# Dealing the gelu passes 2, 3, 3, 0 over the head pairs, and moving y's first low parts behind the third pair's scores

## The chip, the cores and the metric

The kernel runs on one core of one Trainium2 chip. The metric is the device time of one execution in microseconds (us); the median of the runs is compared. The engines are named as the profile names them: PE (TensorE), DVE (VectorE), ACT (ScalarE), POOL (GpSimd) and SP, whose queue issues most of the transfers.

## The reference

A two-layer trunk over 1024 tokens of width 1024, all in float32. The change lies in layer 0, which runs two branches from one input projection:

```python
proj = h @ w_in                      # h = rmsnorm(x)
u_s5, g_s5, q, k, v, g_ret = split(proj)
y = s5(u_s5)                         # diagonal state-space layer, 8 blocks of channels
y = gelu(y)
y = y * sigmoid(y @ glu_w + glu_b)   # the GLU
y_s5 = y * silu(g_s5)
# retention: 8 heads, chunks of 64, per head normalised
scores = einsum('nihd,njhd->nhij', q, k) * decay
out = scores @ v + (q * q_dec) @ S   # S: the state before the chunk
y_ret = norm(out) * silu(g_ret)
x = x + concat(y_s5, y_ret) @ w_out
```

Layer 1 is a convolution module (two projections with a gate, a causal convolution of width 31, a layer norm, an output projection) and a final norm.

## The kernel before

Products keep float32 accuracy by splitting each operand into a high part, rounded for PE, and a low part, the rest. A matmul of 128x128 by 128x512 is issued three times (lines L270 to L272): high by high, high by low, low by high. The high parts are ACT copies, the low parts are subtractions on DVE or POOL.

The program writes the work in one order with priorities, and a scheduler places every instruction in the static order of its engine. A block under `issue_after(x)` is placed behind x; it is a rule for the order. Each engine then runs its list in that order, and waits on semaphores where an operand isn't there. A tile with `bufs=n` gives its next use a free buffer only when the use n before it has been read.

After the front of layer 0 (u, gates, the S5 layer) come four pairs of heads. For a pair, `ret_heads` does: transposes of k (`ktp`) and their decay (`kt`, L1084); products of keys and values (`kv`) and their running state `S` (L1109, L1111), which DVE updates; scores (`sp`, L1118), which DVE masks into `sc` (L1124); products `ro` of q with S (L1145) and of sc with values (L1150); the norm of each head (`st`, `mv`, `rs`, `on`, L1159 to L1165); transposes back (`rt`, L1173); the gate (`grl`, loaded at L1133, multiplied at L1176); and a store to DRAM (`yr_d`, L1179). The k and q projections of the next pair (`mm_k`, `mm_q`), their swapped copies (`kswp`, `qswp`, loaded at L985) and their rotation on POOL and DVE (`krot`, `qrot`) lie between.

Beside the heads the S5 output takes the gelu, in eight passes of 128 channels each (`y_pass`, L919 to L922): a load of `yp` from DRAM on the SP queue, the gelu into `yn` on ACT with its reordering, and a store to `yn_d` issued by ACT. Both tiles have one buffer. Passes 0 and 1 stand with the first pair; 2 and 3, 4 and 5, and 6 and 7 with the next three, each behind the square roots (`rs`) of the pair before.

The GLU then reads y again, in two halves of the tokens. `load_split` loads two blocks of 128 channels into one tile of three buffers (`yf`, L1214), ACT casts the high part (`yh`, L1183), and DVE subtracts the low part (`yl`, L1185). The low parts of the first half (h = 0) are free to go at once; those of the second half stand behind kt of the last pair (the first six blocks) and its masked scores (the last two). For each of the eight output blocks and each half, the GLU loads the S5 gate (`yg`, L1234) and y again (`yn`, L1236), multiplies them on POOL (L1237), runs 24 matmuls (`mm_glu`), a tanh on ACT and a product on DVE (L1242). The scheduler puts the first of these matmuls between the products of the third and fourth pairs. Behind each step of the GLU stand some pieces of `weight_low` (L225 to L230), which loads half a block of the layer-1 weights w_c, forms its low part, and stores it for later (`lows(3)` after each first half, `lows(1)` after each second half, until 14 are done).

Of the kernel before, what the change touches and what calls it, by code (L numbers as in the profile page):

```python
# [11 lines left out]
F32 = mybir.dt.float32  # L12
# [7 lines left out]
P = 128  # L20
# [37 lines left out]
class Trunk:  # L58
# [856 lines left out]
    def y_pass(self, rp, cb):  # L915

        nc = self.nc
        yt = rp.tile([P, 8, P], F32, name=f"yp_{cb}", tag="yp", bufs=1)
        nc.sync.dma_start(yt[:], self.y_d[cb].rearrange("i h g m -> (h g) i m"))  # L919
        yn = rp.tile([P, P, 8], F32, name=f"yn_{cb}", tag="ynt", bufs=1)  # L920
        nc.scalar.activation(yn[:], yt[:].rearrange("p i m -> p m i"), AF.Gelu_apprx_tanh)
        nc.scalar.dma_start(self.yn_d[cb * P:(cb + 1) * P], yn[:].rearrange("p m i -> p (m i)"))  # L922

    def retention(self, st):
        nc, A = self.nc, self.A
        r0 = self.r0 = self.pool("ret0", 1, stack=st)
        early = ExitStack()
        rq = self.rq = self.pool("retq", 1, stack=early, side="right")
        self.vt = [[(r0 if d else rq).tile([P, 4, HALF], F32, name=f"v{d}_{h}") for h in range(2)] for d in range(2)]
        self.rk = rq.tile([P, 2, T], F32, name="ropek")  # L930
        nc.sync.dma_start(self.rk[:], A["rope_k"])
        self.mask = r0.tile([P, NH, P], F32, name="retmask")
        nc.sync.dma_start(self.mask[:], A["ret_mask"])
        self.g128 = r0.tile([P, 4], F32, name="g128")
        nc.sync.dma_start(self.g128[:], A["ret_g128"])
        self.reps = r0.tile([P, NH], F32, name="reteps")
        nc.sync.dma_start(self.reps[:], A["ret_eps"])
        ahead = None
        for pair in range(4):
            cur = list(ahead or self.ret_proj(pair))[-1]  # L940
            if pair == 0:
                with ExitStack() as vst:
                    V = self.ret_values(self.pool("vp", 1, stack=vst))
                self.rp = self.pool("ret", 1, stack=st)
                self.kdec = self.rp.tile([P, NH, 64], F32, name="kdec")
                nc.sync.dma_start(self.kdec[:], A["ret_kdec"])
                ry = self.pool("rety", 1, stack=early, side="right")
            with ExitStack() as held:
                if pair:
                    held.enter_context(self.tc.issue_after(self.last_rs.ins))  # L950
                for cb in (2 * pair, 2 * pair + 1):
                    self.y_pass(ry, cb)

            def turned():
                if pair == 3:
                    early.close()
                    self.lp = self.pool("l1", side="right")
            ahead = pair in AHEAD and self.ret_proj(pair + 1)
            if ahead:
                next(ahead)  # L960
            self.ret_heads(pair, *cur, V, turned)
# [111 lines left out]
    def ret_heads(self, pair, K, Q, qadds, V, turned):  # L1073
        nc, rp = self.nc, self.rp
        v = nc.vector
# [17 lines left out]
        for hf in range(2):  # L1093
            ps = self.bank(f"kv{hf}_{pair}")
            for b4 in range(4):
                b = 4 * hf + b4
# [6 lines left out]
            for b4 in range(4):  # L1103
                b = 4 * hf + b4
# [21 lines left out]
                    self.mask[:, 2 * pair + hh, :].unsqueeze(1).broadcast_to([P, 4, P]), op=ALU.mult)  # L1126


        gts = []
        for hh in range(2):  # L1130
            h = 2 * pair + hh
            gt = rp.tile([P, T], F32, name=f"grl_{h}", tag="grl", bufs=3)
            nc.sync.dma_start(gt[:], self.gr_d[h * P:(h + 1) * P])  # L1133
            gts.append(gt)
        todo = []
        for hf in range(2):
# [17 lines left out]
            for hh in range(2):  # L1154
                h, ps = 2 * pair + hh, pss[hh]
# [21 lines left out]
        for hh in range(2):  # L1177
            h = 2 * pair + hh
# [8 lines left out]
    def layer0_back_and_layer1(self, st):  # L1187
        nc, A = self.nc, self.A
        v, gp = nc.vector, nc.gpsimd
# [7 lines left out]
        def load_split(src, name, halves):  # L1197
            res = [[], []]

            def put(kb, h, f):  # L1200
                a, b = (self.op_tile(self.opA, f"A{h}", f"{name}{q}{kb}_{h}") for q in "hl")
                self.split(f, a, b, v, None if halves or h == 0 else self.last_kt if kb < 6 else self.masked[0])
                res[h].append((a, b))
            for h in range(2):
                for kb in range(KB):
                    if halves:
                        f = lp.tile([P, HALF], F32, name=f"{name}f{kb}_{h}", tag="tp", bufs=TP)[:]
                        nc.sync.dma_start(f, src[rows(kb), hs(h)])
                    else:

                        if kb % 2 == 0:
                            f2 = self.wp.tile([P, 2, HALF], F32, name=f"{name}f{kb}_{h}", tag="wf", bufs=3)
                        f = f2[:, kb % 2, :]
                        nc.sync.dma_start(f, src[rows(kb), hs(h)])  # L1214
                    put(kb, h, f)
            return res
# [8 lines left out]
        def lows(n):  # L1225
            for k in islice(left, n):
                self.weight_low(lp, k, (("cs", "pilot"), ("cq", "sq")), 1)
        ws = {}

        for nb, h in [(nb, h) for nb in range(6) for h in range(2)] + [(6, 0), (7, 0), (6, 1), (7, 1)]:  # L1230
            if h == 0:
                ws[nb] = self.wnext(f"glu{nb}")
            yg = lp.tile([P, HALF], F32, name=f"yg{nb}_{h}", tag="ld", bufs=2)
            nc.sync.dma_start(yg[:], self.gs_d[rows(nb), hs(h)])  # L1234
            yn = lp.tile([P, HALF], F32, name=f"yn{nb}_{h}", tag="ev", bufs=3)
            nc.sync.dma_start(yn[:], self.yn_d[rows(nb), hs(h)])  # L1236
            gp.tensor_tensor(yg[:], yg[:], yn[:], op=ALU.mult)  # L1237
            ps = self.bank(f"mm_glu{nb}_{h}", aux=False)
            self.gemm(ps[:], ws[nb], ys_in[h])
            sg = lp.tile([P, HALF], F32, name=f"sg{nb}_{h}", tag="u", bufs=5)  # L1240
            nc.scalar.activation(sg[:], ps[:], AF.Tanh, scale=0.5, bias=hgb[:, nb:nb + 1])
            v.scalar_tensor_tensor(sg[:], sg[:], 1.0, yg[:], op0=ALU.add, op1=ALU.mult)  # L1242
            if h == 0:
                a, b = (self.op_tile(opB, "B0", f"ys{q}{nb}") for q in "hl")
                nc.scalar.mul(a[:], sg[:], 0.5)
                glu_end = v.scalar_tensor_tensor(b[:], sg[:], 0.5, a[:].bitcast(F32), op0=ALU.mult, op1=ALU.subtract)
                ys0[nb], sg0[nb] = (a, b), sg
                lows(3)
                continue
            yr1 = lp.tile([P, HALF], F32, name=f"yr1_{nb}", tag="tp", bufs=TP)  # L1250
            nc.sync.dma_start(yr1[:], self.yr_d[rows(nb), hs(1)])
            t3f[nb], t2f[nb] = (opB.tile([P, HALF], F32, name=f"{n}_{nb}", tag="B1") for n in ("t3f", "t2f"))
            v.scalar_tensor_tensor(t3f[nb][:], sg[:], -0.5, yr1[:], op0=ALU.mult, op1=ALU.add)
            glu_end = v.scalar_tensor_tensor(t2f[nb][:], sg0.pop(nb)[:], 0.5, t3f[nb][:], op0=ALU.mult, op1=ALU.add)
            lows(1)

        def operand(name, tag, f):
            a, b = (self.op_tile(opB if tag[0] == "B" else self.opA, tag, f"{name}{q}") for q in "hl")
# [498 lines left out]
```

## Time and profile before

| | us |
|---|---|
| median of three runs | 1200.46 |
| lowest and highest of them | 1195.26, 1200.8 |
| the profiled execution | 1199.91 |
| its span, from the first to the last instruction | 1198.1 |
| PE busy in the span | 1167.2 |
| DVE, POOL, ACT busy | 941.0, 687.4, 554.3 |

The granted clock of PE is 0.995 over the span. In the profile a row of a timeline gives start, length, engine, line, operation, output and inputs, the number of instructions merged, and in brackets the idle time before it with what ended it. Line numbers are those of the kernel before.

### The profile page before, as it was taken

What the parts mean: (1) busy time and instruction counts of PE and PEld (TensorE: products, weight loads), DVE (VectorE), ACT (ScalarE), POOL (GpSimd) and SP (SyncE); (2) the same over time, 40 slices, a digit from 0 to 9 for tenths busy, and PEclk for the clock granted to TensorE, in tenths of its full rate; (3) what the DMA queues carried; (4) which work ended last, traced back from release to release, by engine and by line L of the source; (5) the groups of instructions that cost most, each with busy time, mean ns of one, the idle gap of its engine ahead of it and who ended that gap; (6) DMA issues with size and microseconds to landing.
All of it is one profiled execution on the core that took longest, in us unless ns stands there. A gap on an engine that the chain in (4) does not pass through costs nothing.

```text
span 1198.1 us, 17522 instructions
## 1 busy us (share of the span) xinstructions
PE 1167.2 (97%) x6150; PEld 967.8 (81%) x6150; DVE 941.0 (79%) x1529; ACT 554.3 (46%) x833; POOL 687.4 (57%) x489
## 2 busy tenths in 40 slices
PE   8999999999999999988899999999999999999997
PEld 7888878888888888867788888778887887888887
DVE  6875889999617787758788887379999999999643
ACT  7212333332225644233645535367756578444652
POOL 2049979888835133432344034338894678988641
PEclk9999999999999999999999999999999999999999
DMA  9353577788898686664998467866448653456863
GB/s 337 106 182 100 185 265 268 262 275 281 280 299 251 223 280 217 192 211 158 347 325 307 150 228 250 294 229 207 161 152 295 228 178 114 140 188 241 276 247 120
DMA packets 131480, 271.19 MB, mean 226 GB/s; under 512 B 12864, under 2 KB 41792, under 8 KB 131264
## 3 DMA queue, kind: packets, MB, share of 16 engines
q1 hardware_dynamic: 130240, 265.88, 65.8%
q10 hardware_dynamic: 1152, 4.19, 0.9%
q8 instruction: 48, 0.79, 0.3%
q14 instruction: 40, 0.33, 0.1%
HBM read 194.07 MB, written 71.76 MB: 222 GB/s over the span
## 4 chain that ended last, share of the span: by engine, by line
PE 79%; DMA 8%; DVE 7%; POOL 2%; ACT 2%; issue 2%; SPq 1%; DVEq 0%; POOLq 0%; ACTq 0%
PE mm_g L272 7%; PE mm_g L271 7%; PE mm_g L270 6%; PE mm_w L270 3%; PE mm_w L271 3%; PE mm_w L272 3%; PE mm_u L272 2%; PE mm_u L271 2%; PE mm_oc L272 2%; PE mm_oc L270 2%; PE mm_oc L271 2%; PE mm_u L270 2%; PE mm_b L271 2%; PE mm_a L271 2%; PE mm_b L272 2%; PE mm_a L270 2%
## 5 line engine op out<-in xcount | busy, mean ns | idle before, releaser
L1446 DVE SCALAR_TENSOR_TENSOR cv<-u,convw,cv 128x512 f32<-128x512 f32 x358 | 245.2, 748 | 5.7 <-ACT cv L1432 3.9
L1426 POOL TENSOR_TENSOR tp<-tp,tp 128x512 f32<-128x512 f32 x104 | 138.8, 1337 | 33.9 <-ACT tp L1425 28.1
L272 PE MATMUL mm_g<-xh,wl_g 128*128 128x512 f32 x256 | 100.7, 393 | 0.0
L271 PE MATMUL mm_g<-xl,wh_g 128*128 128x512 f32 x256 | 100.6, 393 | 0.0
L270 PE MATMUL mm_g<-xh,wh_g 128*128 128x512 f32 x256 | 100.6, 393 | 0.0
L1425 ACT ACTIVATE tp<-u,convw 128x512 f32<-128x512 f32 x104 | 69.3, 713 | 9.2 <-POOL tp L1426 9.1
L271 PEld LDWEIGHTS mm_g<-xl,wh_g 128*128 128x128 f32 x256 | 48.1, 188 | 11.2 <-issue 1.4
L272 PEld LDWEIGHTS mm_g<-xh,wl_g 128*128 128x128 f32 x256 | 48.1, 188 | 10.4
L270 PEld LDWEIGHTS mm_g<-xh,wh_g 128*128 128x128 f32 x256 | 48.1, 188 | 9.8 <-issue 0.2
L272 PE MATMUL mm_oc<-zh,wl_woc 128*128 128x512 f32 (+1 forms) x152 | 54.7, 360 | 0.1
L270 PE MATMUL mm_oc<-zh,wh_woc 128*128 128x512 f32 (+1 forms) x152 | 54.5, 362 | 0.0
L271 PE MATMUL mm_oc<-zl,wh_woc 128*128 128x512 f32 (+1 forms) x152 | 54.2, 356 | 0.0
L270 PE MATMUL mm_glu<-yh,wh_glu 128*128 128x512 f32 x128 | 50.0, 393 | 2.2 <-ACT yh L1183 2.2
L272 PE MATMUL mm_g<-h1h,wl_cg 128*128 128x512 f32 x128 | 50.0, 390 | 1.1 <-POOL wl_cg L262 1.1
L165 ACT CAST wh_p<-wf_p 128x1024 fp32r<-128x1024 f32 x28 | 29.5, 1054 | 46.2 <-PE mm_w L271 37.6
L270 PE MATMUL mm_u<-xh,wh_u 128*128 128x512 f32 x128 | 49.2, 395 | 1.7 <-ACT wh_u L261 1.7
L271 PE MATMUL mm_b<-h1l,wh_cb 128*128 128x512 f32 x128 | 50.5, 394 | 0.3 <-DVE h1l L1363 0.2
L271 PE MATMUL mm_u<-xl,wh_u 128*128 128x512 f32 x128 | 50.0, 391 | 0.7 <-DVE xl L384 0.6
L272 PE MATMUL mm_a<-h1h,wl_ca 128*128 128x512 f32 x128 | 50.3, 393 | 0.0
L270 PE MATMUL mm_g<-h1h,wh_cg 128*128 128x512 f32 x128 | 50.3, 393 | 0.0
L270 PE MATMUL mm_b<-h1h,wh_cb 128*128 128x512 f32 x128 | 49.9, 390 | 0.4 <-ACT h1h L1362 0.4
L270 PE MATMUL mm_a<-h1h,wh_ca 128*128 128x512 f32 x128 | 50.1, 392 | 0.0
(812 smaller groups left out, 3649.8 us busy)
## 6 DMA issues: line engine op xcount, KB each, us to landing
wf_g<-w_ab SPq DMA_DIRECT2D x16, 512.0 KB, 5.1
a<-w_out SPq DMA_DIRECT2D x32, 256.0 KB, 3.8
ws<-a SPq DMA_DIRECT2D x32, 256.0 KB, 4.5
lf<-w_c SPq DMA_DIRECT2D x32, 256.0 KB, 4.3
wf_p<-ws SPq DMA_DIRECT2D x16, 512.0 KB, 3.7
wf_cb<-w_c SPq DMA_DIRECT2D x16, 512.0 KB, 5.2
wf_ca<-w_c SPq DMA_DIRECT2D x16, 512.0 KB, 4.8
wl_cb<-lo_cb SPq DMA_DIRECT2D x16, 512.0 KB, 3.3
```

Of the source, the lines that this page charges most:

```text
L165: self.nc.scalar.copy(wh[:].rearrange(fl), wf[:])
L270: nc.tensor.matmul(ps, wh[:, kb, :], xh, start=start, stop=False)
L271: nc.tensor.matmul(ps, wh[:, kb, :], xl, start=False, stop=False)
L272: self.last_mm = nc.tensor.matmul(ps, wl[:, kb, :], xh, start=False, stop=stop)
L1425: nc.scalar.mul(sk[:], u[:, k:k + HALF], cw[:, nb, k:k + 1])
L1426: gp.tensor_tensor(s0[:], s0[:], sk[:], op=ALU.add)
L1446: v.scalar_tensor_tensor(dst[:], *tap, accs_[i][:], op0=ALU.mult, op1=ALU.add)
```

## The change

It has four edits. The tile `yp` gets a second buffer, and the passes are dealt to the pairs 2, 3, 3, 0: the second pair's section runs passes 2, 3 and 4, the third's 5, 6 and 7. The gates of a pair's heads are loaded behind the first masked scores of that pair. The low parts of y's first half stand behind the second masked scores of the third pair. The pieces of `weight_low` are two after each first half but the first, and one after each second half of blocks 1 to 5.

```diff
     def y_pass(self, rp, cb):
-        yt = rp.tile([P, 8, P], F32, name=f"yp_{cb}", tag="yp", bufs=1)
+        yt = rp.tile([P, 8, P], F32, name=f"yp_{cb}", tag="yp", bufs=2)
...
-                for cb in (2 * pair, 2 * pair + 1):
+                for cb in ((0, 1), (2, 3, 4), (5, 6, 7), ())[pair]:
                     self.y_pass(ry, cb)
...
+        if pair == 2:
+            self.masked_2 = self.masked[1]
         gts = []
         for hh in range(2):
             h = 2 * pair + hh
             gt = rp.tile([P, T], F32, name=f"grl_{h}", tag="grl", bufs=3)
-            nc.sync.dma_start(gt[:], self.gr_d[h * P:(h + 1) * P])
+            with self.tc.issue_after(self.masked[0].ins):
+                nc.sync.dma_start(gt[:], self.gr_d[h * P:(h + 1) * P])
...
-                self.split(f, a, b, v, None if halves or h == 0 else self.last_kt if kb < 6 else self.masked[0])
+                self.split(f, a, b, v, None if halves else self.masked_2 if h == 0 else self.last_kt if kb < 6 else self.masked[0])
...
-                lows(3)
+                lows(2 if nb else 0)
                 continue
...
-            lows(1)
+            lows(1 if 0 < nb < 6 else 0)
```

The changed program has the same instructions of every kind on PE; their order differs from the third pair's q projection to the GLU's third block, and not behind that.

## Prediction

> **What bounds the kernel now.** I read the page's busy times, then the stages by window, then TensorE's (PE's) waits.
>
> ```profile
> span 1198.1 us, 17522 instructions
> PE 1167.2 (97%) x6150; PEld 967.8 (81%) x6150; DVE 941.0 (79%) x1529; ACT 554.3 (46%) x833; POOL 687.4 (57%) x489
> ```
>
> PE is busy 97% of the span, so time can only come from its gaps, 1198.1 - 1167.2 = 30.9 us in all. The windows (start:end, length, then each engine's busy us; granted clock, DMA share and GB/s last) say which of them this change can reach:
>
> ```profile
> 440.00:520.00 80.00, 80.00 (x534) 67.67 (x533) 56.65 (x161) 27.72 (x27) 34.67 (x22) 1.00 0.67 215
> 520.00:560.00 40.00, 31.59 (x238) 26.54 (x236) 32.26 (x88) 11.51 (x14) 13.02 (x9) 0.91 0.46 142
> 560.00:600.00 40.00, 34.95 (x213) 28.88 (x214) 30.23 (x82) 23.17 (x32) 12.25 (x7) 1.00 0.93 335
> 600.00:640.00 40.00, 40.00 (x178) 33.13 (x177) 33.29 (x36) 14.93 (x25) 20.06 (x11) 1.00 0.94 327
> ```
>
> Pairs one and two (440 to 520) and the GLU's body (from 600) leave PE no gap. The third and fourth pair, with the GLU's first blocks between their heads, lose 8.41 + 5.05 = 13.46 us. PE's waits between 440 and 680 us (total, times, longest) add up to that:
>
> ```profile
> PE sp L1118 <- DVE S L1111: 5.2, 1, 5.2
> PE rt L1173 <- DVE on L1165: 2.6, 2, 1.7
> PE mm_glu L270 <- ACT yh L1183: 2.2, 1, 2.2
> PE ro L1145 <- DVE sc L1124: 1.8, 1, 1.8
> PE kv L1101 <- DVE kt L1084: 1.7, 2, 1.0
> ```
>
> The longest has a second price, seen in PE's timeline (start, length; idle before and its releaser in brackets). The second pair is the undisturbed pattern, the third the disturbed one; the window row gives the clock behind the gap:
>
> ```profile
> 490.29 1.75 PE L1101 MATMUL kv<-v,kt 128*64 128x128 f32 x28
> 495.57 1.04 PE L1118 MATMUL sp<-qrot,krot 64*128 64x128 f32 x13
> 496.46 0.94 PE L1145 MATMUL ro<-S,qrot 64*128 64x128 f32 x11
> 500.40 2.05 PE L1150 MATMUL ro<-v,sc 128*128 128x128 f32 x16
> ...
> 525.58 1.75 PE L1101 MATMUL kv<-v,kt 128*64 128x128 f32 x28 [0.65 <-DVE kt L1084]
> 537.03 1.83 PE L1118 MATMUL sp<-qrot,krot 64*128 64x128 f32 x13 [5.22 <-DVE S L1111]
> 538.77 1.87 PE L1145 MATMUL ro<-S,qrot 64*128 64x128 f32 x11
> ...
> 537.00:541.00 4.00, 3.97 (x29) 3.67 (x30) 4.00 (x9) 0.81 (x1) 1.84 (x2) 0.53 0.01 4
> ```
>
> After the 5.22 us gap the clock is 0.53 and the same work takes 1.83 - 1.04 = 0.79 and 1.87 - 0.94 = 0.93 us longer: 1.7 us. The stage thus loses 13.46 + 1.7 = 15.2 us. [...]
>
> **Why PE waited.** VectorE (DVE), ScalarE (ACT) and the load queue (SP) at that place:
>
> ```profile
> 526.05 2.48 DVE L1185 TENSOR_TENSOR yl<-yf,yh 128x512 fp32r<-128x512 f32 x4
> 535.93 0.69 DVE L1185 TENSOR_TENSOR yl<-yf,yh 128x512 fp32r<-128x512 f32 x1 [6.44 <-ACT yh L1183]
> 536.54 0.34 DVE L1111 SCALAR_TENSOR_TENSOR S<-S,g,kv 128x128 f32<-128x128 f32 x1
> ...
> 535.28 1.23 ACT L1183 CAST yh<-yf 128x512 fp32r<-128x512 f32 x2 [12.19 <-DMA yf<-yn_d]
> ...
> 529.94 1.02 SPq L1214 DMA_DIRECT2D yf<-yn_d x2
> ```
>
> Six low parts of y stand in DVE's order ahead of the third pair's S. The fifth waits for a load issued at 529.94, and S waits with it.
>
> **Part 1: first low parts behind the third pair's masked scores.** In the changed program's order the third pair's S and masked scores (L1124) come directly behind kt and the eight low parts behind them. The third pair then runs as the second did: kv at 525.58, and scores and products (ro) end (500.40 + 2.05) - 490.29 = 12.16 us later, at 537.7. The 5.22 us and the 1.7 us go. Late next are the low parts and what hangs on them (part 4).
>
> **Part 2: passes dealt 2, 3, 3, 0, two buffers.** A pass is one load, one ACT operation and one store:
>
> ```profile
> 507.25 2.10 ACT L921 ACTIVATE yn<-yp 128x1024 f32<-128x1024 f32 x1
> 518.88 1.05 ACT L261 CAST wh_glu<-wf_glu 128x1024 fp32r<-128x1024 f32 x1 [2.06 <-PE mm_k L271]
> 550.58 2.06 ACT L921 ACTIVATE yn<-yp 128x1024 f32<-128x1024 f32 x1
> ...
> DMA to landing us min/median/max: 3.2/5.1/8.9
> ```
>
> The last row is that of all transfers touching yn_d. The result tile keeps one buffer, so each pass still waits for the store before it: 2.1 + 5.1 us a pass. A third pass ends about 7 us after the second. With the second pair it delays the cast of the q weights that the third pair's section uses from 519 us: hidden. With the third section, passes run at 507, 514.5 and 521.7; the last store lands near 529, and the GLU cast at 518.88 moves to about 524, for weights used near 548: hidden too. Without that cover each delay would cost PE its 5 to 7 us. SP is passed by one more yp load in each of these sections, at places where it waits for a gelu anyway. What is won: the last two passes, from 550.58 on, go, y is complete near 529, and the wait of 2.2 us for yh between the fourth pair's products with it.
>
> **Part 3: gates behind the masked scores; fewer low halves of w_c early.** The gate loads (L1133) keep their places in the first three sections: nothing. The low halves (L225 to L230) go from 4, 4, 4, 2 to 0, 3, 3, 3, 3, 2 a block, so the DMA share of 0.93 eases. Their operations on ACT, DVE and SP move into 600 to 680, where DVE is busy 33.29 of 40 and PE full; layer 1 alone reads them, so I count nothing. If DVE had no room there, the five moved subtractions would cost 0.7 us each, 3.5 us.
>
> **Part 4: what is late next.** A GLU matmul step, from the first and last of 24:
>
> ```profile
> 579.24 0.40 PE L270 MATMUL mm_glu<-yh,wh_glu 128*128 128x512 f32 x1
> 584.49 0.39 PE L272 MATMUL mm_glu<-yh,wl_glu 128*128 128x512 f32 x1
> ...
> 533.38 2.49 POOL L991 TENSOR_TENSOR kswp<-kswp,ropek 128x512 f32<-128x512 f32 x2 [10.80 <-DMA kswp<-kraw]
> 518.56 4.58 DVE L992 TENSOR_TENSOR qrot<-qrot,qswp 128x512 f32<-128x512 f32 x2 [5.13 <-POOL qswp L991]
> 551.93 2.64 DVE L1165 TENSOR_SCALAR on<-ro,mv,rs 128x128 f32<-128x128 f32 x8
> 558.09 1.28 DVE L992 TENSOR_TENSOR qrot<-qrot,qswp 128x512 f32<-128x512 f32 x2
> 536.53 1.28 ACT L541 ACT_TABLE_LOAD   x1
> ```
>
> (584.49 - 579.24) / 23 = 0.228 us. Behind ro at 537.7 PE has 17 q matmuls (3.9 us) and a whole first GLU block of 24 (5.5 us), till 547.1; then it transposes the third pair's heads (rt).
> (a) Low parts run from 533, beside POOL's rotation from 533.38. The two qrot rows show what that does to DVE operations on two SBUF tiles: 4.58 us beside POOL, 1.28 without. So the first four end at 535.6 or, slowed, near 539. The y tiles have three buffers, so the second half's first load waits for the fourth low part: it lands 5.1 us later, at 541 or 544. ACT has its cast ahead of the heads' square roots, for which a table is loaded (1.28 us), and eight normalizations follow (2.64): with the casts and roots between, rt can run at 546 or 549.5. PE waits 0 to 2.4 us, with a landing of 8.9 us up to 6; I take 1.5.
> [...]
> (b) Kept: 0.65 before kv, 1.0 before the next kv, and 0.5 and 0.3 for the two rt waits behind (0.9 and 1.7 before). Sum 2.45.
> (c) New: four S operations of the fourth pair and its second scores stand behind the first GLU block's product with its gate (L1242), which waits for POOL's yg, and that for loads queued on SP behind the fourth pair's last gate load:
>
> ```profile
> 559.93 0.85 SPq L1179 DMA_DIRECT2D yr_d<-grl x2
> 568.36 0.32 SPq L1133 DMA_DIRECT2D grl<-gr_d x1
> 571.17 0.44 SPq L1236 DMA_DIRECT2D yn<-yn_d x1
> 576.90 1.54 POOL L1237 TENSOR_TENSOR yg<-yg,yn 128x512 f32<-128x512 f32 x1 [20.26 <-DMA yn<-yn_d]
> ```
>
> PE is at 556.2 at the fourth pair's kv (547.1, rt 0.9, 24 matmuls 5.5, rt, transposes and kt 2.7); kv and the first scores take 3.3 and 29 GLU matmuls 6.6, so it asks for S at 566.1. The third pair's heads are stored (yr_d) near 556; the gate load needs one of them landed, 5 us later (8.4 in the rows), yn goes out near 562, lands 5.1 later, yg takes 1.5, the product and S 0.9: 569.4, a wait of 3.3 us. From the rows' 8.4 it is 6.7, from a landing at 3.2 nearer 1. Then ro waits 1.1 us for the last two low parts, on the same queue.
> Sum left: 1.5 + 2.45 + 3.3 + 1.1 = 8.35 us. Gain 15.2 - 8.35 = 6.9 us. The profiled execution took 1199.91 us (span plus 1.8), 0.55 below the median of 1200.46: **1193.0 us**.
>
> **Rivals.**
> *All waits go* (y lands early, no contention): left are (b) and about 1 us of (c), 3.5 us: gain 11.7, 1188. For it: DMA was busy only 0.46 of 520 to 560. Against: the waits of (c) stand in the written order. Chance 0.2.
> *The wait moves* from S of the third pair to S of the fourth, since that one also stands behind another stage's operand: (c) at 6.7 us with the clock's 1.7, (a) at 2.4 and 1.1 for ro: 14.4 left, about 1199. For it: the row of 8.4 us. Against: fewer low halves on the queues. Chance 0.25.
> *Slower: the y buffers.* Low parts held to 533 free the y tiles 7 to 10 us later than before (526 to 528.5), and every load of the second half waits for one on SP, with qswp, heads' stores and gates queued behind. If these land as the slowest did (8.9): (a) 6, the last y load out at 570, landed 579, ro at 581 against 568.5, 12.5, and 1.7 of clock; with (b) 2.5 and rt waits grown by 1.2, 24 left: 9 slower, 1209. It decides the sign once these waits pass 15.2. Against: DMA showed 0.01 share at 537 to 541. Chance 0.12.
> *No effect* (the order turns out hidden behind the same loads): 1200, 0.05.
>
> **How the numbers follow.** The forecast case holds 0.38. A measurement here tells about 0.5%, 6 us, from no change. Faster by more: the first rival (0.2), 0.3 of the forecast and 0.08 of the second, where stores land sooner: 0.58. Within: the rest of both but 0.02, and no effect: 0.28. Slower: the third and that 0.02: 0.14. Range 1187 (all waits gone and a little more) to 1203 (the second with landings of 8.9).
>
> **What would show it.** Right: in 520 to 560 PE is busy over 37 us with clock 1.00; no PE wait of 5 us at sp of the third pair; no gelu after 530; the longest wait left is sp or ro of the fourth pair on DVE, 2 to 5 us. Wrong: a wait of over 6 us there or at rt of the third pair, DVE idle before yl for yh, or gaps after 600.

## The result and the profile after

The changed kernel took 1184.76 us (median of four runs, 1184.67 to 1188.68) against 1198.04 us for the kernel before on the same chip (four runs, 1195.26 to 1200.8). The ratio is 0.9897, with a 95% interval of 0.9861 to 0.9934: about 13 us, or 1%, faster. The direction was as forecast. The size was not: 6.9 us were forecast, and the measured time lies below the range, which began at 1187.

The profiled execution of the changed kernel took 1188.68 us. Its page begins so:

```profile
span 1186.9 us, 17523 instructions
PE 1166.3 (98%) x6150; PEld 967.2 (81%) x6150; DVE 930.0 (78%) x1529; ACT 554.0 (47%) x833; POOL 690.7 (58%) x489
```

The span is 11.2 us shorter with the same PE work. The two windows of the third and fourth pair (columns as before) now read:

```profile
520.00:560.00 40.00, 37.56 (x286) 31.42 (x284) 36.28 (x93) 15.21 (x23) 15.21 (x9) 1.00 0.58 188
560.00:600.00 40.00, 38.12 (x212) 31.65 (x212) 31.23 (x85) 21.17 (x28) 18.31 (x10) 0.96 0.95 338
```

PE is idle for 2.44 + 1.88 = 4.3 us where it was 13.46. All its waits between 440 and 680 us are three:

```profile
PE mm_glu L270 <- ACT sg L1244: 1.9, 1, 1.9
PE rt L1176 <- DVE on L1168: 1.8, 1, 1.8
PE kv L1101 <- DVE kt L1084: 0.7, 1, 0.7
```

The waits for S (5.2), for yh (2.2) and for sc (1.8) are gone. One is new: the first matmul of the GLU's third block waits 1.9 us for `sg`, the tanh on ACT that reads the PSUM bank (the place its product goes to) it needs. (Lines of the changed kernel are up to three higher than before.) The time from PE's first kv to its first matmul behind the GLU shows that the gain lies in this stage. First the kernel before, then after:

```profile
455.71 1.75 PE L1101 MATMUL kv<-v,kt 128*64 128x128 f32 x28
659.28 0.39 PE L270 MATMUL mm_w<-ysh,wh_p 128*128 128x512 f32 x1
```

```profile
455.25 1.75 PE L1101 MATMUL kv<-v,kt 128*64 128x128 f32 x28
648.60 0.39 PE L270 MATMUL mm_w<-ysh,wh_p 128*128 128x512 f32 x1
```

That is 203.6 us before and 193.4 after: 10.2 of the 11.2 us. In the two later profiles of the changed kernel the same stretch takes 190.9 and 191.4 us.

Where the forecast put its largest remaining wait, S of the fourth pair behind the product with the gate, the rows of SP, POOL, DVE and PE after the change are:

```profile
555.78 0.92 SPq L1182 DMA_DIRECT2D yr_d<-grl  x2
558.42 0.32 SPq L1136 DMA_DIRECT2D grl<-gr_d  x1
559.29 0.42 SPq L1239 DMA_DIRECT2D yn<-yn_d  x1
564.38 1.29 POOL L1240 TENSOR_TENSOR yg<-yg,yn 128x512 f32<-128x512 f32 x1 [8.82 <-DMA yn<-yn_d]
565.71 0.69 DVE L1245 SCALAR_TENSOR_TENSOR sg<-sg,yg 128x512 f32<-128x512 f32 x1 [1.44 <-POOL yg L1240]
566.32 0.34 DVE L1111 SCALAR_TENSOR_TENSOR S<-S,g,kv 128x128 f32<-128x128 f32 x1
566.83 1.04 PE L1118 MATMUL sp<-qrot,krot 64*128 64x128 f32 x13
```

The gate load goes out 2.6 us behind the first of the heads' stores, and the chain behind it is as forecast. S is ready at 566.66, and PE comes for its scores at 566.83, without a wait.

### The profile page after: what moved, and what is told of

Same layout as the page of the kernel before. It is cut to its first block, busy times and chain, and to the rows that moved or that the text cites. A ratio compares the mean times of both kernels' runs of the same rounds, so it can differ in the third digit from the quotient of the medians.

```text
span 1186.9 us, 17523 instructions
## 1 busy us (share of the span) xinstructions
PE 1166.3 (98%) x6150; PEld 967.2 (81%) x6150; DVE 930.0 (78%) x1529; ACT 554.0 (47%) x833; POOL 690.7 (58%) x489
## 4 chain that ended last, share of the span: by engine, by line
PE 80%; DVE 8%; DMA 6%; POOL 2%; issue 2%; SPq 1%; ACT 1%; DVEq 0%; POOLq 0%; ACTq 0%
PE mm_g L272 7%; PE mm_g L271 7%; PE mm_g L270 7%; PE mm_w L270 3%; PE mm_w L271 3%; PE mm_w L272 3%; PE mm_oc L270 2%; PE mm_oc L271 2%; PE mm_oc L272 2%; PE mm_u L272 2%; PE mm_u L271 2%; PE mm_u L270 2%; PE mm_glu L270 2%; PE mm_glu L272 2%; PE mm_glu L271 2%; PE mm_b L271 2%
## 5 line engine op out<-in xcount | busy, mean ns | idle before, releaser
L271 PE MATMUL mm_glu<-yl,wh_glu 128*128 128x512 f32 x128 | 50.6, 396 | 0.0
L272 PE MATMUL mm_glu<-yh,wl_glu 128*128 128x512 f32 x128 | 50.4, 395 | 0.0
L271 PE MATMUL mm_g<-h1l,wh_cg 128*128 128x512 f32 x128 | 50.3, 393 | 0.0
```

The costliest lines, as they stand in the source:

```text
L271: nc.tensor.matmul(ps, wh[:, kb, :], xl, start=False, stop=False)
L272: self.last_mm = nc.tensor.matmul(ps, wl[:, kb, :], xh, start=False, stop=stop)
```

## The experiments

Each kernel was timed against the kernel before on the same chip. The kernels under one heading below share a chip; the kernel before took 1199.27, 1199.18 and 1200.03 us on the three.

### The parts alone

**The kernel after, unchanged** (no diff).

> The changed kernel again, beside the kernel before on one chip. Theory: the gain is the PE waits that the traces show removed between 520 and 600 us, 15.2 us lost before against about 6 after, so 9 to 13 us faster (ratio 0.989 to 0.993), with PE waits left at rt of the third pair (1.8), kv of the fourth (0.7) and mm_glu on sg (1.9). Rival: part of the first measurement was chance between executions, and the gain is nearer the 6.9 us forecast.

Measured: 1185.13 us (1184.1 to 1190.71), ratio 0.9895 (0.9877 to 0.9912): 14.1 us faster (theory 9 to 13), so the first result was not chance. The waits of its profile are sg 1.8, rt 1.0 and kv 0.7.

**Only the first low parts behind the third pair's scores.**

```diff
+        if pair == 2:
+            self.masked_2 = self.masked[1]
...
-  None if halves or h == 0 else self.last_kt ...
+  None if halves else self.masked_2 if h == 0 else self.last_kt ...
```

> Only the low parts of y's first half behind the third pair's masked scores; passes, gates and low halves as before. Theory of waits: the 5.2 us at sp of the third pair and the 1.7 us of low clock go, but y's last two passes still come after the third pair, so a wait for yh near the fourth pair stays or grows: 3 to 7 us faster than before. Rival (the load queue carries the gain, by y and the low halves): under 2 us faster, the wait of 5 us moving to the fourth pair.

Measured: 1199.28 us, ratio 1.0002 (0.9989 to 1.0015): no change, where theory had 3 to 7 us. Its PE waits between 440 and 680 us, but for one of 0.9 at kv:

```profile
PE rt L1175 <- DVE on L1167: 5.5, 2, 5.2
PE mm_glu L270 <- ACT yh L1185: 4.3, 1, 4.3
```

The wait for S went as forecast, and came back as two others, each with slow clock behind it (0.71 over 8 us). PE and ACT say why:

```profile
544.21 1.06 PE L1175 MATMUL rt<-ident,on 128*128 128x128 f32 x8 [0.31 <-DVE on L1167]
550.47 1.97 PE L1175 MATMUL rt<-ident,on 128*128 128x128 f32 x8 [5.20 <-DVE on L1167]
559.49 0.79 PE L270 MATMUL mm_glu<-yh,wh_glu 128*128 128x512 f32 x1 [4.32 <-ACT yh L1185]
...
548.05 1.96 ACT L921 ACTIVATE yn<-yp 128x1024 f32<-128x1024 f32 x1
555.45 1.94 ACT L921 ACTIVATE yn<-yp 128x1024 f32<-128x1024 f32 x1 [5.44 <-DMA yp<-y_d]
```

Between its two groups of transposes rt, PE has nothing to do: the rest of the first 24 GLU matmuls needs the blocks of y that passes 6 and 7 make, and these stand with the fourth pair, at 548 and 555. In the kernel after, y is complete by then, and the GLU's products fill the same place.

**Only the passes dealt 2, 3, 3, 0, with the second buffer.**

```diff
-  ... tag="yp", bufs=1)
+  ... tag="yp", bufs=2)
-                for cb in (2 * pair, 2 * pair + 1):
+                for cb in ((0, 1), (2, 3, 4), (5, 6, 7), ())[pair]:
```

> Only the passes dealt 2, 3, 3, 0 with two buffers. Theory of waits: two masked scores of the third pair still stand behind the fifth to eighth low part, whose load goes out at 529 us, so PE still waits 3 to 5 us in the third pair; only the waits for yh and sc of the fourth pair (2.2 and 1.8) go: 1 to 5 us faster. Rival (the queue): with y complete near 529 most of the gain is there, 8 us or more.

Measured: 1193.32 us, ratio 0.9955 (0.994 to 0.997), 6 us faster (theory 1 to 5). The wait for yh is gone (2.2). The wait for S shrinks from 5.2 to 0.7: in this program's order four low parts stand ahead of S, where a fifth stood ahead of the S that PE waited for, and that fifth, which waits for its y, stands ahead of masked scores. There PE waits now; 1.6 of the 3.3 us lie at the fourth pair, where theory had the wait for sc gone:

```profile
PE ro L1145 <- DVE sc L1124: 3.3, 3, 1.6
PE ro L1150 <- DVE sc L1124: 1.8, 1, 1.8
```

**Both, without the edits of gates and low halves** (the two diffs above).

> Both of these edits, low halves of w_c as before (3 and 1), gates as before (the gate edit leaves every engine's order as it is). Theory of waits: most of the gain, 8 to 11 us; two pieces of low halves stand between the fourth pair's S operations on DVE, so a wait of 0 to 4 us at sp or ro of the fourth pair shows here and not in the whole change. Rival (the queue): without the spread low halves the loads land later, gate product and S later by more than 4 us, gain under 7.

Measured: 1187.6 us, ratio 0.9909 (0.9895 to 0.9923), 11.7 us faster (theory 8 to 11, with a wait at sp or ro of the fourth pair that did not come). Alone the two edits bring 0.0 and 6.0 us, together 11.7: about half of the gain belongs to neither edit but to the pair. The waits left are those of the kernel after: sg 2.0, rt 1.0, kv 0.7. In this trace the stretch from the first kv to the first matmul behind the GLU takes 191.2 us, as in the kernel after. Between the two kernels lie the gates, whose loads stand at the same places of SP's order in both traces, and the low halves; the intervals of the two ratios overlap, so the 2.5 us between their medians are not resolved.

### What is left, and the failed term

**Only the low halves of w_c.**

```diff
-                lows(3)
+                lows(2 if nb else 0)
-            lows(1)
+            lows(1 if 0 < nb < 6 else 0)
```

> The kernel before with only the number of pieces of the low halves of w_c changed (0, 3, 3, 3, 3, 2 a block). Theory of the waits: in the kernel before PE lost nothing to these pieces in 440 to 600 us (its waits there are sp 5.2, rt 2.6, yh 2.2, ro 1.8, kv 1.7), so moving them alone changes the time by less than 1 us: ratio 0.999 to 1.001. Rival (the busy queues: DMA share 0.93 in 560 to 600 us): fewer transfers there land the y loads earlier, and the edit brings the 2.5 us that separate the whole change (1185.1) from the change without it (1187.6) also when it stands alone: ratio 0.997 to 0.9985.

Measured: 1196.87 us, ratio 0.9983 (0.9967 to 1.0): 2.3 us faster, at the edge of what the runs resolve, and nearer to the rival. In the profile the 1.8 us at ro of the fourth pair and one of two waits at rt are gone, but slow clock now stands behind two waits instead of one (0.64 over the 8 us behind S, 0.79 behind yh), so that the stretch from the first kv to the first matmul behind the GLU is only 1.3 us shorter (202.3 against 203.6).

```profile
PE sp L1118 <- DVE S L1111: 5.5, 1, 5.5
PE mm_glu L270 <- ACT yh L1183: 2.3, 1, 2.3
PE kv L1101 <- DVE kt L1084: 1.9, 2, 1.0
PE rt L1173 <- DVE on L1165: 0.9, 1, 0.9
```

**The kernel after with the low halves behind the last square roots.**

```diff
-                self.weight_low(lp, k, ...)
+                with self.tc.issue_after(self.last_rs.ins):
+                    self.weight_low(lp, k, ...)
```

> The kernel after, with every piece of the low halves of w_c placed behind the last square roots (rs) of the heads before it, so that two casts of low halves leave ACT's order ahead of the fourth pair's square roots and of the tanh (sg) that PE waits for. Theory: the wait of 1.8 to 2.0 us of mm_glu for sg (and 1.7 us of slow clock where it follows) comes from ACT's order, casts that wait 2.2 us for their load, and a table load each way; without them the wait goes: 1182 to 1183.5 us, 2 to 3 us faster than the kernel after. Rival: sg is late because the heads' norms on DVE are late, or PE then waits as long at rt of the fourth pair: no change against the kernel after, 1184.5 to 1186.

Measured: 1188.17 us (1187.22 to 1191.88), ratio 0.9909 (0.9888 to 0.993). The mechanism held: the wait for sg is gone, and PE is busy 39.85 of 40 us in 560 to 600. ACT in the kernel after shows what held sg up:

```profile
572.24 1.22 ACT L226 CAST lh<-lf 128x512 fp32r<-128x512 f32 x2 [2.21 <-DMA lf<-w_c]
573.48 1.28 ACT L541 ACT_TABLE_LOAD   x1
...
578.96 1.27 ACT L1244 ACTIVATE sg<-mm_glu,hgb 128x512 f32<-128x512 f32 x2
```

But no time was won. DVE has 86.4 us of work in 600 to 700, where the three profiles of the kernel after have 78.1 to 81.8, and a low part of the next stage's weights is late there. PE's waits between 600 and 780 us begin so; the second is new:

```profile
PE r_ps L536 <- ACT s1q L503: 1.4, 1, 1.4
PE mm_w L272 <- DVE wl_p L166: 1.2, 1, 1.2
```

So 1.8 us went at one place and 1.2 came back at another; the rest is less than the runs spread.

**The kernel after with one buffer for yp.**

```diff
-  ... tag="yp", bufs=2)
+  ... tag="yp", bufs=1)
```

> The kernel after, with one buffer for yp instead of two; passes are still dealt 2, 3, 3, 0. Theory: a pass waits for the store of the one before it (3.7 and 5.1 us in the profile), because the result tile yn has one buffer, and the load of the next yp (about 5 us) fits into the same time; so the second buffer brings nothing: within 1 us of the kernel after, 1184 to 1186. Rival: without the second buffer each pass starts its load only behind the gelu before it, and the load and the store add up: passes end 2 to 5 us later, the GLU's weights and last blocks of y come late, 1187 to 1192.

Measured: 1187.33 us (1184.26 to 1189.7), ratio 0.9893 (0.987 to 0.9916), as the kernel after. The second buffer brings nothing that the runs resolve: a pass waits for its own load instead of for the store ahead of it.

```profile
513.02 2.03 ACT L921 ACTIVATE yn<-yp 128x1024 f32<-128x1024 f32 x1 [4.54 <-DMA yp<-y_d]
520.85 2.09 ACT L921 ACTIVATE yn<-yp 128x1024 f32<-128x1024 f32 x1 [5.79 <-DMA yp<-y_d]
```

Counted from the first pass of the third section (505.44 here), the two start 7.6 and 15.4 us later, against 6.6 to 6.7 and 13.6 to 14.1 in the kernel after. This lag of 0.8 to 1.9 us is smaller than the rival's, and PE has the same three waits (sg 2.5, rt 1.7, kv 0.7).

**The kernel after with the gate load later.**

```diff
             nc.sync.dma_start(self.yr_d[h * P:(h + 1) * P], gts[hh][:])
+            if h == 4:
+                for j in range(2):
+                    nc.sync.dma_start(self.extra_d[j * P:(j + 1) * P], gts[hh][:])
```

> The kernel after, with two more stores of 512 KB (the third pair's first gated head, to a place that nobody reads) behind the real ones, so that the fourth pair's last gate load, which waits for that tile, and the loads of yn and y queued behind it on SP go out later, as if the store had landed later. Theory of the forecast's term (c), with the time the store takes to land as its only error: the product with the gate comes 2 to 4 us later, the second scores and last low parts behind it on DVE too, and PE waits 1.5 to 3.5 us at sp, ro or kv of the fourth pair: 1187 to 1189.5. In its written order all S updates of the pair now stand ahead of that product, so the wait shows at ro rather than at sp. Rival: there is slack between the product and PE, or the scheduler's other order takes it up: 1184 to 1186.5, no wait of the fourth pair's ro above 0.5 us.

Measured: 1185.35 us, ratio 0.9884 (0.9863 to 0.9905): the rival's time. The product with the gate came at 566.47, 11.2 us behind the fourth pair's kv, against 8.7 us in the kernel after (565.71 - 557.00), so 2.5 us later. PE paid 0.8 us for it, over the rival's 0.5:

```profile
566.47 0.69 DVE L1249 SCALAR_TENSOR_TENSOR sg<-sg,yg 128x512 f32<-128x512 f32 x1 [2.42 <-POOL yg L1244]
...
570.07 1.16 PE L1149 MATMUL ro<-S,qrot 64*128 64x128 f32 x14 [0.81 <-DVE sc L1125]
```

The test is not clean, since the scheduler put all S updates ahead of the product once the load was late. ACT's order changed too, and the wait for sg is gone, so the time of the whole says nothing of the price. What it shows is that the chain of term (c) exists, and that a third of a delay reached PE in that order. What it would cost in the order of the kernel after was not tried.

### Contention, passes, and the clock

**Two, and four, of the first low parts ahead of the third pair's S.**

```diff
-  None if halves else self.masked_2 if h == 0 else ...
+  None if halves or (h == 0 and kb < 2) else self.masked_2 if h == 0 else ...   # or kb < 4
```

> The kernel after, with the first two of y's first low parts free to go ahead of the third pair's S, as all of them were before; the other six stay behind the masked scores. Theory of the forecast's term (a): the wait of 1.0 to 1.8 us at rt of the third pair comes from DVE, which works through eight low parts in 533 to 543 us at 1.4 us each beside POOL's rotation; two of them run at 525 to 527 us, where DVE is idle for 1.7 us, and rt comes 1.5 to 2 us sooner: 1183 to 1184.5 us, 1 to 2 us faster than the kernel after on the same chip, rt wait under 0.5 us, no new wait at sp or ro of the third pair. Rival: S of the third pair, or the square roots behind the last cast of y (ACT, waiting for its load), bound rt anyway: no change, within 0.7 us of the kernel after.

> The same with the first four low parts ahead of the third pair's S. Theory: the casts end at 526.6 us, the four low parts near 527.5 to 528, so S comes 1.5 to 2 us later; with the deal alone S at 528.0 cost 0.7 us at sp. So rt's wait goes (1 to 1.8 us), and 0.5 to 1 us comes back at sp or ro of the third pair: 0 to 1 us faster than the kernel after, and not faster than with two ahead. Rival (the order of low parts and scores costs PE nothing once y is early): as with two ahead or better.

Measured: 1187.17 us (two) and 1186.17 us (four), ratios 0.9892 (0.9872 to 0.9912) and 0.9884 (0.9866 to 0.9901). Neither can be told from the kernel after. With two ahead the wait at rt stayed at 1.1 us, and theory missed: the four low parts behind the scores still ran beside POOL and took 6.10 us, and a wait for sg of 2.6 stood behind. With four ahead rt's wait fell to 0.6, and S of the third pair cost 0.8, as expected.

**The second buffer given to yn.**

```diff
-  ... tag="yp", bufs=2)
+  ... tag="yp", bufs=1)
-  ... tag="ynt", bufs=1)
+  ... tag="ynt", bufs=2)
```

> The kernel after, with the second buffer given to the result tile yn instead of yp. Theory: a pass then waits no longer for the store before it, only for its own load; the second pair's and third pair's third pass end about 2 to 4 us sooner (before 519 instead of 523 us). That frees ACT for the cast of the GLU weights and the casts of y, which nobody on PE waits for at that place: within 1 us of the kernel after. Rival: earlier casts let the low parts and the second half of y start earlier, and rt's wait of 1.0 to 1.8 us goes: 1 to 2 us faster.

Measured: 1187.92 us, ratio 0.9895 (0.9878 to 0.9912), no change. The theory's step failed: passes did not end sooner. They began 8.2 and 15.4 us behind the first (513.50 and 520.75), later than in the kernel after, because they now waited 5.1 and 5.2 us for their own loads. Two buffers for both tiles at once, which a pass would need to overlap the one ahead of it, were not tried.

**The kernel after again.**

> The kernel after once more, on the chip of the three runs beside it, for their comparison and for the slow clock behind short waits. Theory: a wait of PE of 1.2 to 2.5 us is followed by about 1.7 us of slow clock in some executions and not in others, whatever its length in that span (behind 1.88 us it came, behind 1.83, 1.96 and 2.55 us it didn't; behind the wait of 1.2 us in layer 1 it came in seven profiles of ten). So the same kernel again takes 1184 to 1190 us, and its profile has the slow clock behind one, two or none of its waits of 1.2 us and over, with span less the waits unchanged. Rival: the slow clock goes with the length of the wait, so that a wait of 1.8 us behaves as in the first profile of this kernel, with clock 0.8 in the 8 us behind it.

Measured: 1188.81 us (1185.64 to 1191.19), ratio 0.9901 (0.9885 to 0.9918). The theory held. The profiled execution took 1185.64 us, 3.0 less than the first profile of the same kernel, with the same waits (rt 1.8, sg 1.7, kv 0.7). The difference is the clock. The windows of 8 us behind the waits for sg and, in layer 1, for the square sum (1.2 us), first profile:

```profile
579.70:587.70 8.00, 8.00 (x32) 6.48 (x33) 5.10 (x20) 7.89 (x10) 3.33 (x3) 0.79 1.05 409
896.94:904.94 8.00, 8.00 (x34) 6.55 (x35) 6.09 (x12) 2.83 (x5) 3.49 (x2) 0.79 0.92 294
```

and the same two windows of this one:

```profile
578.86:586.86 8.00, 8.00 (x39) 6.71 (x40) 5.08 (x20) 7.89 (x10) 2.85 (x3) 1.00 1.04 390
895.47:903.47 8.00, 8.00 (x41) 6.58 (x42) 7.63 (x14) 4.41 (x6) 3.52 (x2) 1.00 0.89 297
```

A clock of 0.79 over 8 us is 1.7 us of PE time, twice: 3.4 us. None of the versions tried beats the kernel after by more than the runs spread; the three medians of that one kernel on three chips, 1184.76, 1185.13 and 1188.81, span more than all its variants do.

## Why the prediction was right in direction and too small

**Part 1 (low parts behind the scores): right, but not alone.** The 5.22 us and its slow clock went, and the third pair ran as the second. (Of the six low parts that the forecast saw ahead of S, five stood ahead of the S operation that PE waited for.) That this needs y early is not in the forecast, which priced parts 1 and 2 as separate sums. The run of part 1 alone shows it: 0.0 us.

**Part 2 (the deal): right, and too small.** Passes ran at 506.8, 513.4 and 520.9 us (forecast 507, 514.5, 521.7) and the wait for yh went. It is worth 6.0 us alone and 11.7 with part 1, not 2.2, since it also lets the GLU fill the third pair and takes loads of y out of the fourth pair's queue (next point).

**Part 4, term (c): the step that failed.** It left 3.3 us at S and 1.1 us at ro of the fourth pair; both measured nothing. The chain was right, and one link was mis-sized: the landing of the head's store that the gate load waits for, 5 us in the forecast and 2.6 measured. The forecast put it between 3.2 and the 8.4 of its own rows. In the kernel before, the rows of the second pair's stores and of the third pair's, up to the gate load behind each:

```profile
523.76 0.92 SPq L1179 DMA_DIRECT2D yr_d<-grl  x2
526.43 0.32 SPq L1133 DMA_DIRECT2D grl<-gr_d  x1
...
557.61 2.22 SPq L1214 DMA_DIRECT2D yf<-yn_d  x5
559.93 0.85 SPq L1179 DMA_DIRECT2D yr_d<-grl  x2
565.26 0.32 SPq L1214 DMA_DIRECT2D yf<-yn_d  x1
568.36 0.32 SPq L1133 DMA_DIRECT2D grl<-gr_d  x1
```

SP's waits from 550 to 572 us, and the landing times of the third pair's two stores:

```profile
SPq L1214 <- DMA yn_d<-yn: 4.7, 2, 4.5
...
SPq L1133 <- DMA yr_d<-grl: 2.8, 1, 2.8
...
DMA to landing us min/median/max: 8.4/9.2/9.9
```

and the landing times of the same two stores in the kernel after:

```profile
DMA to landing us min/median/max: 2.6/3.3/4.0
```

The 8.4 us were a true landing: the gate load's wait of 2.8 us ends with it, and the y load at 565.26 adds nothing. But this store went out behind five loads of y (256 KB each) that had not landed, and SP had held these for 4.5 us, up to 557.61, for the store of a late pass. The second pair's store had nothing ahead of it and landed in 2.6 us: the right size stood in the forecast's own trace. With the deal the y loads are through before the third pair's stores. The other kernels agree: the first of these stores lands in 7.3 us with only the low halves changed (five y loads ahead), in 5.4 with only the scores (two), and in 2.6 in the ten profiles with the deal whose gate load follows these stores alone (none). With 2.6 us the forecast's own chain gives S at 567.0 (569.4 less 2.4), against 566.66 in the trace, and a wait of 0.9 us, not 3.3.

**Part 4, term (a): right.** 1.5 us forecast at rt of the third pair, 1.8, 1.0 and 1.8 measured in three profiles of the kernel. Its cause is seen in DVE and POOL of the kernel after:

```profile
531.87 6.77 DVE L1188 TENSOR_TENSOR yl<-yf,yh 128x512 fp32r<-128x512 f32 x4
...
531.77 2.95 POOL L991 TENSOR_TENSOR kswp<-kswp,ropek 128x512 f32<-128x512 f32 x2 [4.83 <-DMA kswp<-kraw]
534.69 3.41 POOL L989 TENSOR_TENSOR krot<-kraw,ropek 128x512 f32<-128x512 f32 x2
```

Four low parts took 2.48 us before, with POOL idle (0.00 us busy from 526.00 to 528.50), and 6.77 beside POOL, which was busy all the while (6.73 us of 531.87 to 538.60): a factor of 2.7. That price decided little: PE lost 1.8 us where the low parts took 4.3 longer.

**Term (b): too large.** 2.45 us forecast, 0.7 measured: the wait before the fourth pair's kv kept 0.7 of its 1.0, and those before the third pair's kv and at the later rt did not remain.

**Not foreseen.** The wait for sg (1.3 to 2.6 us in eight profiles with the deal and the scores), which comes from ACT's order behind the fourth pair (it went when two casts left that order), and the 1.7 us of slow clock that follow it in some executions. Of the forecast's signs, those on the third pair came; the last did not, as the longest wait left is not S or ro of the fourth pair but sg.

**The sum.** The forecast left 8.35 us of 15.2. Measured were 4.3 us of waits and, in the profiled execution, 1.7 of clock at this place: 6.0 left, so 9.2 of the stage's 10.2 us. In the other two profiles of this kernel 3.5 and 4.1 us were left, without slow clock, and the stage was 12.7 and 12.1 us shorter than before. So term (c), with its 4.4 us, is the largest of the differences to the forecast. About 1 us isn't in these rows in any of the three, and its cause stays open. The rival in which all waits go, 1188 us with 3.5 left, came nearest, and had a chance of 0.2; the two cases that rest on term (c) were given 0.63 together. That the time lies below the range has a second reason: the kernel before, too, was 2.4 us faster beside the result (1198.04) than when the forecast was made (1200.46). **Part 3:** no run changes the gates alone, and no trace shows them doing anything. The low halves were priced at nothing: alone they brought 2.3 us, at the edge of what the runs resolve, and a gain on top of the other edits is not shown.

## What to carry to other kernels

A landing time read off a trace belongs to the transfers that were under way there (2.6 and 8.4 us for stores of one size here): ask which of them the change moves, and look in the same trace for a transfer of the same kind with nothing ahead of it. Where one edit makes work available (y early) and another makes the place for it (low parts late), price the pair and not the parts, by asking at each gap that an edit moves what PE would do there, and whether its operands exist by then. And a wait of one or two microseconds has a second price that comes in some executions and not in others (1.7 us of PE time behind the square sum, in nine profiles of fourteen), so that single profiles of such variants can't be ranked by their spans.

## What the runs showed of the hardware

**Slow clock behind short waits, in some executions.** The wait of 1.2 us for the square sum is in all fourteen profiles of this case. In nine of them the 8 us behind it run at 0.79, in five at 1.00. Behind the wait for sg it was two of eight (behind 1.88 and 2.57 us, not behind 1.83, 1.96 or 2.55). Behind waits of 4.3 to 5.5 us the clock fell in four of four (0.53 in the 4 us behind the 5.22 us of the kernel before, 0.64 to 0.71 in the 8 us behind the others), and behind the one of 1.1 us for the weights of layer 1 in none of six (the kernels before and after, the kernel after again, two and four ahead, and the second buffer of yn). Where it falls, it goes to 0.50 for 3.41 us, as in the kernel after from 580.92 and from 898.36, or twice that, as in the kernel before from 533.94 to 540.77. Windows of 1 us of the kernel after:

```profile
581.00:582.00 1.00, 1.00 (x4) 0.78 (x3) 1.00 (x3) 0.99 (x3) 0.00 (x0) 0.50 1.03 406
...
584.00:585.00 1.00, 1.00 (x5) 0.84 (x4) 0.00 (x0) 0.97 (x3) 1.00 (x1) 0.83 1.07 412
```

Here the fall comes 1.2 us after PE has resumed (579.70), and behind the square sum of the same profile 1.4 us after (896.94). In the kernel before it came while PE still waited for S, 3.1 us ahead of its first scores (537.03). In both profiles the slow stretches begin whole multiples of 3.413 us apart: 317.44 us in the kernel after (93 times; 580.92 and 898.36), and 655.36 in the kernel before (192 times; 533.94 and 1189.30). So the moment of the fall is not set by the wait alone. What decides whether a wait is followed by slow clock is not shown: for the square sum, waits of 1.22 and 1.23 us were (the kernel after, four ahead, the second buffer of yn) and waits of 1.24 and 1.25 us were not (the kernel before, the kernel after again, two ahead), and neither were the longer ones of 1.96 and 2.55 us for sg.

**A head's store of 512 KB landed in 2.6 us** when no other transfer was under way at its issue (DMA share 0.00 from 552.50 to 555.78 in the kernel after): 2.6 us for the first store of the third pair in ten profiles with the deal. Behind two loads of 256 KB it took 5.4, behind five 7.3 and 8.4. The median over all eight stores is 6.4 in the kernel before and 5.5 in the kernel after.
